# First conditioning chunks formed as columns, rotary tables made early, context keys moved behind u

## The chip, the core and the metric

The kernel runs on one core of a Trainium2 chip. The core has a matrix engine (TensorE, "PE" in the profile, with its weight loads as "PEld"), a vector engine (VectorE, DVE), an activation engine (ScalarE, ACT), a general engine (GpSimd, POOL) and a queue engine that issues the loads (SyncE, SP). They run side by side, each works through its own list of instructions in order, and they wait for each other by semaphores. The metric is the time of one execution on the device in microseconds (us). TensorE's clock has two levels, 1.2 and 2.4 GHz; the profile shows which of them was granted.

## The reference, cut to what matters

The model has two layers over 1024 tokens of width 1024, with a context of 256 tokens. Layer 0 is attention beside a spatial gating MLP, layer 1 a convolution module, and a SwiGLU FFN follows each. Every sub-layer is scaled and shifted by a conditioning vector (adaLN). The change lies in the beginning of layer 0:

```
def adaln(cvec, w_mod, b_mod):
    return jnp.split(jax.nn.silu(cvec) @ w_mod + b_mod, 6, axis=-1)
...
        sh1, sc1, gt1, sh2, sc2, gt2 = [t[:, None, :] for t in adaln(c, w_mod[l], b_mod[l])]
        xm = rms_norm(h, g_mix[l]) * (1.0 + sc1) + sh1
        if even or ctx_after:
            csh1, csc1, cgt1, csh2, csc2, cgt2 = adaln(c_ctx, w_mod[l], b_mod[l])
            xc = rms_norm(hc, g_mix[l]) * (1.0 + csc1) + csh1
...
    q, k, v, su, sv = split_in_proj(xm @ w_in)
    q = apply_axial_rope(rms_norm(q.reshape(b, n, N_Q_HEADS, HEAD_DIM), q_gain), rope)
    k = apply_axial_rope(rms_norm(k.reshape(b, n, N_KV_HEADS, HEAD_DIM), k_gain), rope)
```

Nothing of layer 0 can be projected before sh1 and sc1 are known: 2048 numbers each for `c` and for `c_ctx`, from an 8 MB part of `w_mod`.

## The kernel before

All activations lie transposed: 128 rows of the width on the partitions, tokens along the free side, the tokens in two halves A and B of 512. Each f32 operand of a large product is split into a high part (rounded to the engine's f32r format, on ACT, L112) and a low part (the rest, on DVE, L113), and a product is three matmuls over those parts (`mm3`, L175 to L181).

The beginning goes so. SP loads, in this order, the eight blocks of `w_mod` for sh1 and sc1 (`wma`, one 128 x 2048 block for each 128 rows k of the conditioning vector), half A of x among them (`xA`), then the first weights (`raw`), the context (`xc`) and half B (`xB`). For each block k, the two conditioning columns `s2v[:, k, :]` (for `c` and `c_ctx`) are multiplied with the block. Of its four chunks of 512 columns three go to TensorE, with the two conditioning columns as the stationary side, into three PSUM rows `mps` (L277). The fourth is done on DVE: it adds the block, weighted per partition, to two tiles `macc` (L278, L279, L254, L256), and TensorE sums these over partitions with a column of ones (L283 to L285). ACT copies the three rows out (`mrow`, L305), TensorE turns them into columns with 12 small transposes (L308), and all lands in `mcol`, 128 partitions x 16 columns x 2. DVE then makes the shift and scale (`mod`, `modc`, `gp`, L310 to L313), and half A, which was normalized meanwhile (`rbA`, L288), is shifted and split into `xm` (L387 to L403).

Then TensorE forms, in program order, keys and values of half A (`kv_tile` 2 to 5, tile `kvps`), of the context (0 and 1, from `xcm`), the first 256 columns of u for half A (`su_half(0, wu, 0)`, tile `ups`), keys and values of half B (6 to 9), u for half B, then queries (`qps`) and so on. Keys are turned by rotary tables `kC`, `kS` (`table`, L378, on POOL). Meanwhile DVE forms the later conditioning chunks (`adaln_group`: tile `acc` from `wmb` loads through a ring of three buffers, which the tiles of the sums of squares share).

The order of instructions on each engine is set at build time by the framework's scheduler, which starts from the order of the code and from its own estimate of when operands are there; so a small edit moves rows on every engine. Weight tiles `w` have four buffers, and blocks 4 to 7 of `wma` use the same four: a later weight can be split only when TensorE has finished with the block in its buffer.

Of the kernel before, what the change touches and what calls it, by code (L numbers as in the profile page):

```python
# [14 lines left out]
AF = mybir.ActivationFunctionType  # L15
ALU = mybir.AluOpType
AX = mybir.AxisListType

P = 128
D = 1024  # L20
KD = D // P
# [6 lines left out]
HD = 64  # L28
# [24 lines left out]
def hybrid_kernel(  # L53
# [19 lines left out]
    nc = tc.nc  # L73
# [15 lines left out]
    def htile(name="h", n=HALF):  # L89
        return hpool.tile([P, NB], F32, name=name, tag="h")[:, 0:n]  # L90
# [4 lines left out]
    def xtile(n=HALF, name="x"):  # L95
        return xpool.tile([P, NB], F32, name=name, tag="x")[:, 0:n]

    def blk(name="blk", dtype=F32R, n=HALF):
        return blkp.tile([P, 2, NB], dtype, name=name, tag="blk")[:, :, 0:n]

    def psa(n=HALF, name="psa"):
        return pa.tile([P, HALF], F32, name=name, tag="a")[:, 0:n]

    def psc(n=HALF, name="psc"):
        return pcn.tile([P, HALF], F32, name=name, tag="c")[:, 0:n]
# [15 lines left out]
    ident = const.tile([P, P], F32, name="ident")  # L121
# [27 lines left out]
    def prep(src):  # L149
        out = []  # L150
        for j in range(2):
            raw = load_raw(src[:, j * 1024:(j + 1) * 1024])
            w = wpool.tile([P, 2, 1024], F32R, name="w", tag="w")
            split(w[:, 0, :], w[:, 1, :], raw)
            out.append(w)
        return out
# [5 lines left out]
    def next_w():  # L162
        if not wready:
            wready.append(prep(wqueue.popleft()))
        w = wready.popleft()
        if wqueue:
            wready.append(prep(wqueue.popleft()))
        return w

    def w_rhs(w, k, c0=0, c1=256):  # L170
        t = w[k // 4]
        o = (k % 4) * 256
        return t[:, 0, o + c0:o + c1], t[:, 1, o + c0:o + c1]

    def mm3(ps, pairs):  # L175
        n = len(pairs) * 3
        i = 0
        for lh, ll, rh, rl in pairs:
            for a, b in ((lh, rh), (lh, rl), (ll, rh)):
                nc.tensor.matmul(out=ps, lhsT=a, rhs=b, start=(i == 0), stop=(i == n - 1))  # L180
                i += 1  # L181

    def col_sums(out, a):

        nc.tensor.matmul(out=out, lhsT=a, rhs=ones[:, 0:1], start=True, stop=True)


    def rstd_bcast(s, n, scale):

        at = [min(o, n - P) for o in range(0, n, P)]  # L190
        nj = len(at)
        ps = psc(nj, "ps_v")
        for j, o in enumerate(at):
            col_sums(ps[:, j:j + 1], s[:, o:o + P])
        v = sm(nj, "nv")
        nc.vector.tensor_scalar(out=v, in0=ps, scalar1=scale, scalar2=EPS, op0=ALU.mult, op1=ALU.add)  # L196
        r = rsqrt_small(v, nj, "nr")
        rb = psc(n, "rb")
        for j, o in enumerate(at):
            nc.tensor.matmul(out=rb[:, o:o + P], lhsT=r[:, j:j + 1].broadcast_to([P, P]), rhs=ident, start=True, stop=True)  # L200
        return rb

    def sumsq(tiles, n, alloc=ntile):
        s = None
        for t in tiles:
            q = alloc(n, "sq")
            nc.scalar.activation(q, t, AF.Square)
            if s is None:
                s = q
            else:  # L210
                nc.vector.tensor_tensor(out=s, in0=s, in1=q, op=ALU.add)
        return s
# [3 lines left out]
    def new_xm(half):  # L216
        xm[half] = [blk("xm") for _ in range(KD)]
# [15 lines left out]
    def load_pairs(half, k0, n):  # L233
        out = []
        for k in range(k0, k0 + n):
            if k % 2 == 0:
                t = blk("xp", F32)
            nc.sync.dma_start(out=t[:, k % 2, :], in_=xT[half, k])
            out.append(t[:, k % 2, :])
        return out  # L240
# [5 lines left out]
    s2 = const.tile([P, 16], F32, name="s2")  # L246
    nc.scalar.activation(s2, col(C_C2, 16), AF.Silu)
    s2v = s2.rearrange("p (k two) -> p k two", two=2)
    mps = [psa(name="mps") for _ in range(3)]
    macc = [xtile(name="macc") for _ in range(2)]  # L250

    def weighted_add(acc, w, cs, first):
        if first:
            nc.vector.tensor_scalar(out=acc, in0=w, scalar1=cs, scalar2=None, op0=ALU.mult)  # L254
        else:
            nc.vector.scalar_tensor_tensor(out=acc, in0=w, scalar=cs, in1=acc, op0=ALU.mult, op1=ALU.add)  # L256

    xA = []
    for k in range(KD):
        if k < 4:  # L260
            ws = []
            for i in range(2):
                t = blk("wma", F32)
                nc.sync.dma_start(out=t, in_=wm_a[k][:, i * 1024:(i + 1) * 1024].rearrange("p (a b) -> p a b", a=2))
                ws += [t[:, 0, :], t[:, 1, :]]
        else:
            t = wpool.tile([P, 2048], F32, name="wma", tag="w")
            nc.sync.dma_start(out=t, in_=wm_a[k])
            ws = [t[:, j * 512:(j + 1) * 512] for j in range(4)]
        if k in (1, 3):  # L270
            xA += load_pairs(0, 2 * (k - 1), 4)
        if k == 5:
            wqueue.append(w_in[2])
            wqueue.extend(w_in[{"q": 0, "u": 3, "v": 5}[kind] + g] for kind, g in STAGES)
            wqueue.extend(w_out[g] for _ in range(2) for g in range(4))
        for j in range(3):
            nc.tensor.matmul(out=mps[j][0:2, :], lhsT=s2v[:, k, :], rhs=ws[j], start=(k == 0), stop=(k == KD - 1))  # L277
        for e in range(2):  # L278
            weighted_add(macc[e], ws[3], s2v[:, k, e:e + 1], k == 0)  # L279
        if k == 4:  # L280
            rbA = rstd_bcast(sumsq(xA, HALF), HALF, 1.0 / D)
    mcol = psc(32, "mcol")
    for i in range(4):  # L283
        for e in range(2):
            col_sums(mcol[:, 24 + 2 * i + e:25 + 2 * i + e], macc[e][:, i * P:(i + 1) * P])  # L285
    wready.append(prep(wqueue.popleft()))
    for t in xA:
        nc.vector.tensor_tensor(out=t, in0=t, in1=rbA, op=ALU.mult)  # L288
# [1 line left out]
    for j in range(2):  # L290
        t = blk("xc", F32)
# [7 lines left out]
        nc.vector.scalar_tensor_tensor(out=gp[:, dst:dst + 8], in0=sc, scalar=1.0, in1=col(g, 8),  # L299
                                       op0=ALU.add, op1=ALU.mult)  # L300

    mrow = []
    for j in range(3):
        t = htile("mrow")
        nc.scalar.activation(t[0:2, :], mps[j][0:2, :], AF.Copy)  # L305
        mrow.append(t)
    for i in range(12):
        nc.tensor.transpose(mcol[:, 2 * i:2 * i + 2], mrow[i // 4][0:2, (i % 4) * P:(i % 4 + 1) * P], ident[0:2, 0:2])  # L308
    mcv = mcol.rearrange("p (i two) -> p i two", two=2)
    nc.vector.tensor_tensor(out=mod[:, 0:16], in0=mcv[:, :, 0], in1=col(C_BMOD, 16), op=ALU.add)  # L310
    nc.vector.tensor_tensor(out=modc, in0=mcv[:, :, 1], in1=col(C_BMOD, 16), op=ALU.add)
# [54 lines left out]
    kst2 = kvpool.tile([P, 2, NKT * P], F32R, name="kst2")  # L366
    v1 = kvpool.tile([P, NKT * 2, P], F32R, name="v1")
    v2 = kvpool.tile([P, NKT * 2, HD], F32R, name="v2")

    gt = htile("gt")  # L370
    nc.sync.dma_start(out=gt[:, 0:256], in_=gains.partition_broadcast(P))
    rt = []
    for i in range(2):
        t = htile("rt")
        nc.sync.dma_start(out=t, in_=rope[i])
        rt.append(t)

    def table(i, g):  # L378
        t = htile("tab")
        nc.gpsimd.tensor_tensor(out=t.rearrange("p (t d) -> p t d", d=HD),  # L380
                                in0=rt[i].rearrange("p (t d) -> p t d", d=HD),
                                in1=gt[:, g * HD:(g + 1) * HD].unsqueeze(1).broadcast_to([P, 8, HD]), op=ALU.mult)
        return t

    new_xm(0)

    def shift(k):  # L387
# [6 lines left out]
    def parts(k):  # L394
        t = xm[0][k]
        tc.keep_in_program_order(nc.scalar.activation(t[:, 0, :], xA[k], AF.Copy))
        nc.vector.tensor_tensor(out=t[:, 1, :], in0=xA[k], in1=t[:, 0, :].bitcast(F32), op=ALU.subtract)

    for k in range(0, KD, 2):
        shift(k)  # L400
        shift(k + 1)
        parts(k + 1)
        parts(k)  # L403
    kC, kS, qC, qS = table(0, 2), table(1, 3), table(0, 0), table(1, 1)
    xcm = [blk("xcm") for _ in range(4)]

    def xc_dst(k):
# [43 lines left out]
    def flush(n=0):  # L451
        while len(later) > n:
            later.popleft()()
# [44 lines left out]
    def su_half(g, wsu, half):  # L498
        for j in range(2):
            ps = psa(name="ups")  # L500
            mm3(ps, [(*w_rhs(wsu, k, j * P, (j + 1) * P), xm[half][k][:, 0, :], xm[half][k][:, 1, :])
                     for k in range(KD)])
            u = htile("u")
            nc.scalar.activation(u, ps, AF.Gelu_apprx_tanh)
            ut[2 * g + j, half] = u
# [10 lines left out]
    for kt in range(2, 6):  # L516
        kv_tile(kt)
    flush()
    for kt in range(0, 2):
        kv_tile(kt)  # L520
    flush()
    wu = next_w()
    su_half(0, wu, 0)
    for kt in range(6, 10):
        kv_tile(kt)
    flush()
# [212 lines left out]
    for n in range(len(steps) + LAG):  # L739
        if n < len(steps):  # L740
            i, kt = steps[n]
            while i not in prepped:
                next(bg)
            half, pair, e = units[i]
# [14 lines left out]
        i, kt = steps[n - LAG]  # L759
        half, pair, e = units[i]  # L760
# [33 lines left out]
    for half in range(2):  # L794
# [5 lines left out]
        for k in range(KD):  # L800
            t = htile("h")
# [399 lines left out]
```

## Time and profile before

| | |
|---|---|
| median of 3 runs | 2373.87 us (2371.97 to 2375.66) |
| profiled execution | 2372.76 us, its span 2371.0 us, mean granted clock 0.99 |
| busy of the span | PE 98%, PEld 83%, DVE 69%, ACT 39%, POOL 17% |

The span runs from the first to the last instruction; the profiled execution's own time is 1.76 us more. A busy PE is one with a matmul in flight. A matmul of this kernel in plain f32 leaves two records, called passes here: 24 matmuls into `mps` are 48 records.

### The profile page before, as it was taken

Reading aid. Unit: us, or ns where it says so; the run is one execution under the profiler, and the core shown is the slowest. Engines: PE = TensorE matmul, PEld = TensorE weight load, DVE = VectorE, ACT = ScalarE, POOL = GpSimd, SP = SyncE. Lnnn points to the kernel's source line nnn. Section 1 sums busy time; section 2 is a strip of 40 time slices with the busy share of each in tenths; the row PEclk is TensorE's granted clock in tenths of the full one; section 3 lists DMA queues with packets and bytes.
Section 4 is the critical chain, followed back from the end, with each engine's and each line's share of the span. In section 5 each row is a group of like instructions: output and inputs, shape, how many; then the busy total and the mean of one; then the engine's idle time right before and its main releaser. Section 6 shows DMA issues by size and latency. Waiting matters only on the chain.

```text
span 2371.0 us, 31670 instructions
## 1 busy us (share of the span) xinstructions
PE 2327.0 (98%) x12396; PEld 1978.2 (83%) x12396; DVE 1628.5 (69%) x2515; ACT 918.5 (39%) x1480; POOL 411.1 (17%) x405
## 2 busy tenths in 40 slices
PE   7999899999999999999999999999999999999998
PEld 3899677777888888888888788888878989999998
DVE  6887777656545666447999966999986555444357
ACT  4542688843211222234333455333445433222222
POOL 2362677820000000001112300002230000000000
PEclk9899999999999999999999999999999999999999
DMA  8451000042222455332222242222233222222222
GB/s 307 136 194 55 19 1 1 6 148 96 101 77 89 160 194 174 121 126 88 94 93 89 91 166 98 89 98 90 97 98 121 96 96 89 90 90 89 90 90 98
DMA packets 79573, 245.68 MB, mean 104 GB/s; under 512 B 8512, under 2 KB 12864, under 8 KB 78912
## 3 DMA queue, kind: packets, MB, share of 16 engines
q1 hardware_dynamic: 79424, 243.66, 30.4%
q8 instruction: 97, 1.59, 0.3%
q14 instruction: 52, 0.43, 0.1%
HBM read 235.24 MB, written 8.39 MB: 103 GB/s over the span
## 4 chain that ended last, share of the span: by engine, by line
PE 73%; DVE 12%; issue 2%; POOL 1%; ACT 1%; DMA 0%; DVEq 0%; ACTq 0%; POOLq 0%
PE gu L180 35%; PE fo L180 17%; PE pw L180 8%; DVE conv L999 7%; PE wo L180 4%; DVE w L113 2%; PE mx L628 2%; PE st L650 1%; PE st L649 1%; PE o L676 1%; PE o L674 1%; PE o L675 1%; POOL pacc L993 1%; DVE h L791 0%; DVE conv L1002 0%
## 5 line engine op out<-in xcount | busy, mean ns | idle before, releaser
L180 PE MATMUL gu<-xm,w 128*128 128x512 f32 (+2 forms) x5280 | 997.8, 350 | 1.9 <-ACT xm L226 1.9
L180 PEld LDWEIGHTS gu<-xm,w 128*128 128x128 f32 x5280 | 854.4, 188 | 135.0 <-ACT xm L226 2.1
L112 ACT ACTIVATE w<-raw 128x1024 fp32r<-128x1024 f32 x324 | 340.6, 1056 | 556.7 <-issue 237.7
L113 DVE TENSOR_TENSOR w<-raw,w 128x1024 fp32r<-128x1024 f32 x324 | 406.8, 1259 | 192.4 <-ACT w L112 191.8
L180 PE MATMUL fo<-act,w 128*128 128x512 f32 (+2 forms) x2640 | 499.8, 350 | 1.5 <-DVE act L113 1.5
L180 PEld LDWEIGHTS fo<-act,w 128*128 128x128 f32 x2640 | 428.3, 189 | 65.7 <-DVE act L113 1.9
L999 DVE SCALAR_TENSOR_TENSOR conv<-glu,pc,conv 128x496 f32<-128x496 f32 (+1 forms) x400 | 316.6, 836 | 0.3
L791 DVE SCALAR_TENSOR_TENSOR h<-fo,mod,h 128x264 f32<-128x264 f32 (+2 forms) x256 | 159.6, 631 | 96.7 <-PE fo L180 95.9
L993 POOL TENSOR_TENSOR pacc<-pacc,ptmp 128x496 f32<-128x496 f32 (+1 forms) x64 | 109.0, 1703 | 450.7 <-ACT pacc L989 398.3
L180 PE MATMUL pw<-xm,w 128*128 128x512 f32 x768 | 178.7, 394 | 0.0
L180 PEld LDWEIGHTS pw<-xm,w 128*128 128x128 f32 x768 | 144.1, 188 | 33.5
L841 DVE TENSOR_TENSOR silu<-gu,silu 128x512 f32<-128x512 f32 (+2 forms) x110 | 63.8, 580 | 141.0 <-PE gu L180 140.8
L840 ACT ACTIVATE silu<-gu 128x512 f32<-128x512 f32 (+2 forms) x110 | 56.2, 511 | 260.4 <-PE gu L180 260.4
L140 POOL TENSOR_TENSOR nr<-nv,mhalf 128x4 f32<-128x4 f32 (+2 forms) x16 | 16.4, 1027 | 803.3 <-DVE nv L196 803.3
L630 DVE TENSOR_REDUCE mp<-mx 128x1 f32<-128x512 f32 (+1 forms) x192 | 112.1, 598 | 24.6 <-PE mx L628 21.6
L112 ACT ACTIVATE act<-silu 128x512 fp32r<-128x512 f32 (+2 forms) x110 | 59.1, 537 | 143.6 <-DVE silu L841 143.6
L665 POOL TENSOR_TENSOR pb<-p,pb 128x512 fp32r<-128x512 f32 x80 | 104.3, 1304 | 5.3
L256 DVE SCALAR_TENSOR_TENSOR acc<-raw,s,acc 128x512 f32<-128x512 f32 x84 | 62.9, 749 | 45.2 <-DMA raw<-in_wm_b_dram 44.1
L180 PE MATMUL pw<-sw,w 128*128 128x264 f32 (+1 forms) x576 | 91.4, 320 | 0.0
L180 PE MATMUL wo<-cat,w 128*128 128x512 f32 x384 | 89.9, 394 | 0.7 <-DVE cat L113 0.7
L969 POOL MEMSET glu<- 128x15 f32 x16 | 0.9, 112 | 510.6 <-PE fo L180 510.6
L180 PEld LDWEIGHTS pw<-sw,w 128*128 128x128 f32 x576 | 83.0, 188 | 7.2
(169 smaller groups left out, 2450.3 us busy)
## 6 DMA issues: line engine op xcount, KB each, us to landing
raw<-in_ffn_in_dram SPq DMA_DIRECT2D x164, 512.0 KB, 3.6
raw<-in_ffn_out_dram SPq DMA_DIRECT2D x82, 512.0 KB, 3.6
raw<-in_wm_b_dram SPq DMA_DIRECT2D x48, 512.0 KB, 3.7
raw<-in_pw_dram SPq DMA_DIRECT2D x48, 512.0 KB, 3.7
wmb<-in_wm_b_dram SPq DMA_DIRECT2D x64, 256.0 KB, 2.8
raw<-in_w_out_dram SPq DMA_DIRECT2D x16, 512.0 KB, 3.6
raw<-in_w_in_dram SPq DMA_DIRECT2D x14, 512.0 KB, 4.6
wma<-in_wm_a_dram SPq DMA_DIRECT2D x8, 512.0 KB, 7.9
```

What stands on the lines that cost most here:

```text
L112: nc.scalar.activation(dst_hi, src, AF.Copy)
L113: nc.vector.tensor_tensor(out=dst_lo, in0=src, in1=dst_hi.bitcast(F32), op=ALU.subtract)
L180: nc.tensor.matmul(out=ps, lhsT=a, rhs=b, start=(i == 0), stop=(i == n - 1))
L256: nc.vector.scalar_tensor_tensor(out=acc, in0=w, scalar=cs, in1=acc, op0=ALU.mult, op1=ALU.add)
L628: pin(nc.tensor.matmul(out=ps, lhsT=b[:, 0, j * P:(j + 1) * P], rhs=kst1[:, kv, o:o + n], start=True, stop=True))
L630: chained(nc.vector.tensor_reduce(out=mp[:, 3 * j + s:3 * j + s + 1], in_=ps, axis=AX.X, op=ALU.max))
L665: chained(eng.tensor_tensor(out=t[:, 1, :], in0=p, in1=t[:, 0, :].bitcast(F32), op=ALU.subtract))
L791: nc.vector.scalar_tensor_tensor(out=h, in0=ps, scalar=gc, in1=h, op0=ALU.mult, op1=ALU.add)
L840: nc.scalar.activation(sg, ps, AF.Silu)
L841: nc.vector.tensor_tensor(out=sg, in0=ps, in1=sg, op=ALU.mult)
L993: nc.gpsimd.tensor_tensor(out=pacc, in0=pacc, in1=tmp, op=ALU.add)
L999: nc.vector.scalar_tensor_tensor(out=out, in0=g[:, t:t + n], scalar=wc(t), in1=out, op0=ALU.mult, op1=ALU.add)
```

## The change

It makes three edits. First, all 16 blocks of 128 columns of each `wma` block become the stationary side of a matmul, with the two conditioning columns as the moving side, so that TensorE writes columns into `mcol` at once: 16 matmuls with 2 moving columns for each k, 128 in all. The rows `mps`, the DVE tiles `macc`, the copies `mrow`, the transposes and the sums with ones go. Second, gains and rope are loaded, and the four rotary tables made, in step k = 1 of that loop. Third, the context's two key and value tiles come behind u of the first half.

```
-    mps = [psa(name="mps") for _ in range(3)]
-    macc = [xtile(name="macc") for _ in range(2)]
+    mcol = psc(32, "mcol")
...
+        if k == 1:
+            gt = htile("gt")
+            nc.sync.dma_start(out=gt[:, 0:256], in_=gains.partition_broadcast(P))
+            rt = []
+            for i in range(2):
+                t = htile("rt")
+                nc.sync.dma_start(out=t, in_=rope[i])
+                rt.append(t)
+            kC, kS, qC, qS = table(0, 2), table(1, 3), table(0, 0), table(1, 1)
...
-        for j in range(3):
-            nc.tensor.matmul(out=mps[j][0:2, :], lhsT=s2v[:, k, :], rhs=ws[j], start=(k == 0), stop=(k == KD - 1))
-        for e in range(2):
-            weighted_add(macc[e], ws[3], s2v[:, k, e:e + 1], k == 0)
...
+        for i in range(16):
+            nc.tensor.matmul(out=mcol[:, 2 * i:2 * i + 2], lhsT=ws[i // 4][:, (i % 4) * P:(i % 4 + 1) * P],
+                             rhs=s2v[:, k, :], start=(k == 0 and i == 0), stop=(k == KD - 1),
+                             skip_group_check=True)
...
-    mcol = psc(32, "mcol")
-    for i in range(4):
-        for e in range(2):
-            col_sums(mcol[:, 24 + 2 * i + e:25 + 2 * i + e], macc[e][:, i * P:(i + 1) * P])
...
-    mrow = []
-    for j in range(3):
-        t = htile("mrow")
-        nc.scalar.activation(t[0:2, :], mps[j][0:2, :], AF.Copy)
-        mrow.append(t)
-    for i in range(12):
-        nc.tensor.transpose(mcol[:, 2 * i:2 * i + 2], mrow[i // 4][0:2, (i % 4) * P:(i % 4 + 1) * P], ident[0:2, 0:2])
...
-    gt = htile("gt")
-    nc.sync.dma_start(out=gt[:, 0:256], in_=gains.partition_broadcast(P))
...
-    kC, kS, qC, qS = table(0, 2), table(1, 3), table(0, 0), table(1, 1)
...
+    wu = next_w()
+    su_half(0, wu, 0)
     for kt in range(0, 2):
         kv_tile(kt)
     flush()
-    wu = next_w()
-    su_half(0, wu, 0)
```

On TensorE the first rows were these, up to the first keys (names as above; `ps_v` and `rb` are the sum and the broadcast of a normalization, here that of half A; x counts matmuls that follow each other):

```order
L277 MATMUL mps<-wma,s_101 2x512 x12
L185 MATMUL ps_v<-ones,sq 128x1 x4
L277 MATMUL mps<-wma,s_101 2x512 x3
L200 MATMUL rb<-ident,nr 128x128 x4
L277 MATMUL mps<-wma,s_101 2x512 x9
L185 MATMUL mcol<-ones,macc 128x1 x8
L308 MATMUL mcol<-ident,mrow 128x2 x12
L180 MATMUL kvps<-w,xm 128x256 x30
```

and are now these (the two `ps_v` rows behind the first are those of the context and of half B):

```order
L296 MATMUL mcol<-s_101,wma 128x2 x80
L185 MATMUL ps_v<-ones,sq 128x1 x4
L296 MATMUL mcol<-s_101,wma 128x2 x15
L200 MATMUL rb<-ident,nr 128x128 x4
L296 MATMUL mcol<-s_101,wma 128x2 x33
L185 MATMUL ps_v<-ones,sq 128x1 x2
L180 MATMUL kvps<-w,xm 128x256 x8
L180 MATMUL ups<-xm,w 128x512
L200 MATMUL rb<-ident,nr 128x128 x2
L185 MATMUL ps_v<-ones,sq 128x1 x4
L180 MATMUL kvps<-w,xm 128x256 x72
```

24 wide matmuls, 8 sums and 12 transposes have become 128 matmuls of 2 columns; the normalization of half A stands in the same place among the blocks.

On DVE, around the making of `mod`, there stood before:

```order
L288 TENSOR_TENSOR xp<-xp,rb 128x512 x8
L256 SCALAR_TENSOR_TENSOR macc<-wma,s_101,macc 128x512 x2
L113 TENSOR_TENSOR w<-raw,w 128x1024 x2
L211 TENSOR_TENSOR sq<-sq 128x256 x2
L310 TENSOR_TENSOR mod<-mcol,pc 128x16
```

and now:

```order
L303 TENSOR_TENSOR xp<-xp,rb 128x512 x8
L211 TENSOR_TENSOR sq<-sq 128x512
L113 TENSOR_TENSOR w<-raw,w 128x1024
L211 TENSOR_TENSOR sq<-sq 128x512
L113 TENSOR_TENSOR w<-raw,w 128x1024
L211 TENSOR_TENSOR sq<-sq 128x512 x2
L253 TENSOR_SCALAR acc<-wmb,s_101 128x512
L318 TENSOR_TENSOR mod<-mcol,pc 128x16
```

The sums of squares of half B (`sq`, 128x512), two weight splits and the first step of a later conditioning chunk (`acc`, which needs a `wmb` load) stand ahead of `mod` now. That load is issued on SP behind the sixth `raw` load, and it waits for the last of those `sq` rows, whose buffer it takes.

Further down on DVE, the low parts of half B (`xm<-xp,mod,xm`) stood before like this:

```order
L225 SCALAR_TENSOR_TENSOR xp<-xp,gp,rb 128x512 x8
L256 SCALAR_TENSOR_TENSOR acc<-wmb,s_101,acc 128x512
L426 TENSOR_REDUCE ss<-kr 128x2
L113 TENSOR_TENSOR v_298<-kvps,v_297 128x64
L254 TENSOR_SCALAR acc<-wmb,s_101 128x512
L445 TENSOR_TENSOR qn<-qn,tab 128x128
L227 SCALAR_TENSOR_TENSOR xm<-xp,mod,xm 128x512 x5
```

and now the second of them has this ahead of it:

```order
L417 TENSOR_REDUCE ss<-kr 128x2
L255 SCALAR_TENSOR_TENSOR acc<-wmb,s_101,acc 128x512
L419 TENSOR_SCALAR hv<-ss 128x2
L436 TENSOR_TENSOR qn<-qn,tab 128x128
L437 TENSOR_TENSOR kr<-qn,kr 128x128
L255 SCALAR_TENSOR_TENSOR acc<-wmb,s_101,acc 128x512
L417 TENSOR_REDUCE ss<-kr 128x2
L113 TENSOR_TENSOR v_369<-kvps,v_368 128x64
L255 SCALAR_TENSOR_TENSOR acc<-wmb,s_101,acc 128x512
L436 TENSOR_TENSOR qn<-qn,tab 128x128
L419 TENSOR_SCALAR hv<-ss 128x2
L227 SCALAR_TENSOR_TENSOR xm<-xp,mod,xm 128x512
```

Between the normalized half B (`xp<-xp,gp,rb`) and the second of its eight low parts there are ten `acc` steps now; before, two stood ahead of the first five low parts. Behind the first queries TensorE's rows are the same as before.

## Rows read from the trace of the kernel before

**Rows 1.** The page: its first line, the span.

```profile
span 2371.0 us, 31670 instructions
```

**Rows 2.** Stretches: start:end, length, busy us (xcount) of each engine, granted clock, DMA.

```profile
28.90:42.40 13.50, 12.00 (x55) 5.09 (x54) 11.66 (x23) 6.25 (x12) 0.00 (x0) 1.00 1.04 405
42.60:49.30 6.70, 5.14 (x24) 5.14 (x25) 6.12 (x13) 6.70 (x14) 4.33 (x1) 0.50 0.51 200
...
63.80:68.80 5.00, 5.00 (x22) 4.77 (x22) 5.00 (x18) 2.15 (x8) 0.00 (x0) 0.50 0.16 50
68.80:70.60 1.80, 1.80 (x9) 1.77 (x8) 1.03 (x5) 0.45 (x2) 0.53 (x1) 0.50 0.37 125
70.60:76.60 6.00, 5.33 (x25) 5.24 (x26) 3.86 (x10) 1.37 (x6) 3.31 (x7) 0.50 0.55 186
76.70:113.00 36.30, 36.30 (x219) 31.85 (x218) 32.02 (x75) 19.91 (x53) 15.06 (x25) 1.00 0.42 138
```

**Rows 3.** Timeline of PE, 5 to 46 us: start, us, instruction, xcount [idle before].

```profile
5.94 8.20 PE L277 MATMUL mps<-wma,s 128*2 128x512 f32 x12 [5.94 <-DMA wma<-in_wm_a_dram]
...
30.30 7.89 PE L277 MATMUL mps<-wma,s 128*2 128x512 f32 x18
38.12 1.95 PE L185 MATMUL mcol<-ones,macc 128*128 128x1 f32 x16
...
44.16 6.13 PE L180 MATMUL kvps<-w,xm 128*128 128x256 f32 x30 [3.26 <-ACT xm L396]
```

**Rows 4.** Timeline of PE, 63 to 77 us.

```profile
63.75 5.12 PE L180 MATMUL kvps<-w,xcm 128*128 128x256 f32 x22 [2.57 <-DVE xcm L227]
68.86 1.84 PE L185 MATMUL ps_v<-ones,sq 128*128 128x1 f32 x8
...
75.60 1.55 PE L200 MATMUL rb<-ident,nr 128*128 128x128 f32 x8
```

**Rows 5.** Passes with one moving column: shortest/median/longest ns, first and last start.

```profile
L185 PE MATMUL ps_v<-ones,sq x112: 164/250/353, 23.9 to 2361.5; 128*128 128x1 f32 x112
```

**Rows 6.** Timeline of PE, first queries and what follows.

```profile
112.97 4.17 PE L180 MATMUL qps<-w,xm 128*128 128x256 f32 x33
...
136.73 23.04 PE L180 MATMUL qps<-w,xm 128*128 128x256 f32 x192
...
159.96 22.48 PE L180 MATMUL ups<-xm,w 128*128 128x512 f32 x96
```

**Rows 7.** Timeline of DVE and POOL around the making of mod.

```profile
40.94 0.17 DVE L310 TENSOR_TENSOR mod<-mcol,pc 128x16 f32<-128x16 f32 x1 [0.95 <-PE mcol L308]
44.97 10.11 POOL L380 TENSOR_TENSOR tab<-rt,gt 128x512 f32<-128x512 f32 x4 [17.96 <-DMA rt<-in_rope_dram]
```

**Rows 8.** Groups of ACT and DVE, 0 to 45 us: busy us, mean ns | idle before.

```profile
L112 ACT ACTIVATE w<-raw 128x1024 fp32r<-128x1024 f32 x2 | 2.1, 1058 | 10.3 <-DMA raw<-in_w_in_dram 10.3
L207 ACT ACTIVATE sq<-xp 128x512 f32<-128x512 f32 x8 | 5.0, 629 | 14.2 <-DMA xp<-in_xT_dram 13.7 <-DVE sq L211 0.2
L113 DVE TENSOR_TENSOR w<-raw,w 128x1024 fp32r<-128x1024 f32 x2 | 2.4, 1220 | 0.0
L256 DVE SCALAR_TENSOR_TENSOR macc<-wma,s,macc 128x512 f32<-128x512 f32 x14 | 9.9, 748 | 6.6 <-DMA wma<-in_wm_a_dram 6.6
```

**Rows 9.** DMA issues: xcount, KB each, median us from issue to landing.

```profile
wmb<-in_wm_b_dram SPq DMA_DIRECT2D x64, 256.0 KB, 2.8
raw<-in_w_in_dram SPq DMA_DIRECT2D x14, 512.0 KB, 4.6
```

**Rows 10.** Timeline of SP and DVE: the third raw load's issue, a sq, the acc steps.

```profile
37.42 0.33 SPq L146 DMA_DIRECT2D raw<-in_w_in_dram  x1
...
68.04 0.68 DVE L211 TENSOR_TENSOR sq<-sq 128x512 f32<-128x512 f32 x1
...
69.43 0.49 DVE L254 TENSOR_SCALAR acc<-wmb,s 128x512 f32<-128x512 f32 x1
...
73.83 0.75 DVE L256 SCALAR_TENSOR_TENSOR acc<-wmb,s,acc 128x512 f32<-128x512 f32 x1 [1.12 <-DMA wmb<-in_wm_b_dram]
```

More of the change, by code (lines that the diff above doesn't have):

```diff
@@ L258, in hybrid_kernel, with table @@
     xA = []
+    def table(i, g):
+        t = htile("tab")
+        nc.gpsimd.tensor_tensor(out=t.rearrange("p (t d) -> p t d", d=HD),
+                                in0=rt[i].rearrange("p (t d) -> p t d", d=HD),
+                                in1=gt[:, g * HD:(g + 1) * HD].unsqueeze(1).broadcast_to([P, 8, HD]), op=ALU.mult)
+        return t
     for k in range(KD):
@@ L368, in hybrid_kernel @@
     v2 = kvpool.tile([P, NKT * 2, HD], F32R, name="v2")
-    gt = htile("gt")
-    nc.sync.dma_start(out=gt[:, 0:256], in_=gains.partition_broadcast(P))
[L372 to L383, printed above, removed]
     new_xm(0)
```

## The prediction, made before the changed kernel ran

> **What bounds the kernel now.** I read the page first: a span of 2371.0 us [rows 1], to which the profiled execution adds 1.76, 2372.76 in all. The busy shares of the page say little, because TensorE is waited for nearly everywhere. So I asked for stretches of the beginning. From 76.7 us TensorE is busy without a break and at the full clock [rows 2], and the first queries start at 112.97 [rows 6]. Behind them TensorE's rows are unchanged. So what the change is worth is the shift of one event, the first query, and I cost everything ahead of it.
>
> Ahead of it there are two parts. Up to 40.94, where `mod` is made [rows 7], the conditioning chunks are formed. Keys start at 44.16 [rows 3], 3.2 us behind `mod`. From there to the first query it takes 68.8 us. How much of that is work? At the full clock a key or query pass costs 23.04 / 192 = 0.120 us and a u pass 22.48 / 96 = 0.234 [rows 6]. The stretch holds 240 passes for keys and values, 96 for u and some 40 narrow ones (norms, transposes) at about 0.11 (below): 28.8 + 22.5 + 4.3, say 55 us. So 14 us are lost to waits (2.57 us for the context's low parts alone [rows 4]) and to the half clock, which was granted from 42.6 to 49.3 and from 63.8 to 76.6 [rows 2].
>
> **The new conditioning part.** 24 wide matmuls are replaced by 128 with two moving columns. They are plain f32, so 256 passes, each with 128x128 weights of its own. The trace has this form with one moving column. Eight such passes took 1.84 us at the half clock; the longest such pass of the trace lasted 0.353, so one starts every (1.84 - 0.353) / 7 = 0.213 us. At the full clock 16 took 1.95, with a median of 0.250, so one every 0.113 [rows 3 to 5]. These are the two bounds of the price. A second column is another column of streaming, which I neglect.
>
> Here the Trainium skill can be weighed against the rows. "TensorE: Matmul & The Clock Gate", section on LDWEIGHTS, gives a load by its columns alone, an estimate of 107 ns for 128 columns. By that the passes would cost 27 us at either level. The rows agree at 2.4 GHz (0.113) and not at 1.2 GHz (0.213).
>
> So the granted clock decides. At the start it is the half one: the first twelve passes of `mps` took 8.20 us, eighteen later ones 7.89 [rows 3]. Then wide passes raised it. Would narrow ones? From 63.75 to 70.7 TensorE worked almost without a gap, 22 recorded key passes of 256 columns and then the eight narrow ones [rows 4], and the clock stayed at 0.50 [rows 2]. From 44.16 on, 256-column passes without the narrow ones raised it within 5.2 us, and from 71 to 76.6 key passes and eight passes of 128 columns did too [rows 2, 4]. And before 42.4 it was full under `mps`, and fell after narrow sums, small transposes and a wait of 3.26 us [rows 2, 3]. I take it that narrow passes don't raise it, so the price is 0.213.
>
> The order on TensorE puts 8 `ps_v` and 8 `rb` passes among the 256, which run at the same half clock and price. Thus the columns are ready at 5.94 + 272 x 0.213 = 63.9 us, against 40.9 before: **+23.0**. No load holds this up: the gains and rope loads (128 KB and twice 256 KB by their shapes) ahead of block 2 take 1.6 us at the 405 GB/s of rows 2, and TensorE, which came to block 7 at 30.30 + 12 x 0.44 = 35.6 before [rows 3], now does at 57.1.
>
> What goes is worth little here. DVE loses 16 `macc` steps of about 0.7 us [rows 8], and ACT its copies, but these lay beside loads and TensorE. The tables' 10.1 us on POOL [rows 7] move from 45 to 55 us into a time when POOL has nothing to do.
>
> **From the columns to the keys.** `mod` now stands on DVE behind `acc`. That needs the first `wmb` load, which waits for the last `sq` of half B, and that one stands behind a weight split whose buffer TensorE frees 32 passes before the end, at 57.1. From there: split on ACT 1.06, low part on DVE 1.22, `sq` add 0.68, square 0.63, add 0.68 [rows 8, 10] make 61.4; load 2.8 [rows 9], `acc` 0.49 [rows 10]: 64.7. That is **+0.8** behind the columns (bounds: 0 if the load is early, 3.8 if it starts only when the columns are ready). With 3.2 us from `mod` to the keys as before, keys start at 68.0.
>
> **From the keys to the first query.** 55 us of work at the full clock. TensorE comes to it at half clock. Before, the first such spell lasted 5.2 us behind the first key and the second 13.7, of which half each is lost. Now the first nine key and u matmuls are followed by twelve passes for norms, eight of them narrow, so I take 9 us at half, **4.5** lost (bounds 2.6 and 6.8, half of each spell). Context keys behind u no longer wait for `xcm`: DVE has its low parts ready some 10 us before. What is late next is half B. Ten `acc` steps now stand between its normalization and its second low part. Half B's `rb` stands behind some 80 key passes, at about 85 us; eight steps of 0.68 (taken as long as the `sq` add) bring DVE to 90. With three buffers, load 2.8 and step 0.75 [rows 9, 10], three `acc` steps take 3.6 us at best; three loads have landed by then, the other seven steps take some 9 us, and each waits in the same row of instructions for keys to be finished. So the low parts come at 102 to 108, and TensorE asks at 103 (the first query less 96 key passes and 48 of u): **2.5** (bounds 0, since before there was no such wait, and 5). Together 68.0 + 55 + 4.5 + 2.5 = 130, against 112.97, or 17 us later. The second part gains 7 us of the 14 lost; the first loses 24.
>
> **The sum.** 2372.76 + 17 = 2389.8. The profiled execution lies 1.1 below the median, which is within the runs' own spread, so I forecast **2390**.
>
> **Rivals.**
> First, the clock does rise under narrow passes. The Trainium skill says so if read plainly: "TensorE: Matmul & The Clock Gate", in the table under "Why this matters for your kernels", asks only that TensorE be kept busy without a pause. No row here has a long run of narrow passes, so only the 1.84 us in rows 4 speak against it. Then, with 27 passes at half until about 11.7, the columns are ready at 5.94 + 27 x 0.213 + 245 x 0.113 = 39.4. But then the load of `wmb` decides: the third `raw` load, issued at 37.42 before [rows 10] and now 1.6 later for the rope, lands at some 43.6 with 4.6 us of landing [rows 9]; split, sums, load and `acc` as above (1.06 + 1.22 + 1.99 + 2.8 + 0.49) make 51.2, keys at 54.4, the first query at 54.4 + 55 + 5 = 114.4. That gives +1.5, **2374**: no difference. The point from which it decides is the pass time: below about 0.15 us the change is no longer slower.
> Second, on the faster side, the clock rises and the load of `wmb` is early: keys at 39.4 + 3.2 = 42.6, the first query at 42.6 + 55 + 3 = 100.6, so **2360**. Against it speaks the order on DVE and SP, where `sq` and the sixth `raw` load come first.
> Third, slower than forecast: the wait for half B lets the clock fall once more, as after the 3.26 us in rows 3; 5 us of wait and 3 at half clock give **2396**.
>
> **How the numbers follow.** About 0.2%, 4.7 us, is what a measurement of this kernel can tell. Half clock, the forecast: 0.84, the third rival within it (0.12). The first rival: 0.12, most of it within 0.2%. The second: 0.04, faster. So faster 0.04, same 0.11, slower 0.85. With the bounds (0 to 3.8, 2.6 to 6.8, 0 to 5) the forecast's case reaches from 2385 to 2397; a clock that rises for part of the run lies below. I give 2378 to 2398, which leaves out the two fast rivals.
>
> **What would show it.** Right: granted clock 0.50 until some 70 us, `mcol` passes every 0.213, the last at 64, keys at 68, the first query near 130, and the same distances behind it. Wrong: `mcol` passes every 0.113, or `mod` waiting for a `wmb` load for long, or half B's low parts in time. If the first query comes before 118, my reading of the clock has failed.

## The result, and the profile after

The changed kernel took 2388.9 us (median of 4 runs, 2388.30 to 2390.72), the kernel before in the same session 2372.97 (2371.97 to 2375.66): ratio 1.0067, 95% interval 1.0049 to 1.0084. It is 15.9 us slower. The forecast was 2390, and slower.

The profiled execution has this span, on the page's first line; it is 16.0 us longer than before's [rows 1]:

```profile
span 2387.0 us, 31992 instructions
```

The timeline of TensorE up to the first query (start, us, instruction, xcount, idle before) answers to [rows 3, 4, 6]:

```profile
5.45 34.26 PE L296 MATMUL mcol<-s,wma 128*128 128x2 f32 x160 [5.45 <-DMA wma<-in_wm_a_dram]
...
49.53 14.08 PE L296 MATMUL mcol<-s,wma 128*128 128x2 f32 x66
...
66.50 2.08 PE L180 MATMUL kvps<-w,xm 128*128 128x256 f32 x8 [2.04 <-ACT xm L388]
...
70.44 8.79 PE L180 MATMUL kvps<-w,xm 128*128 128x256 f32 x72
...
87.99 5.82 PE L180 MATMUL ups<-xm,w 128*128 128x512 f32 x24 [0.69 <-ACT u L495]
...
94.50 4.73 PE L180 MATMUL kvps<-w,xcm 128*128 128x256 f32 x38 [0.69 <-ACT u L495]
...
102.88 0.62 PE L180 MATMUL kvps<-w,xm 128*128 128x256 f32 x3 [1.78 <-DVE xm L227]
...
103.87 6.20 PE L180 MATMUL kvps<-w,xm 128*128 128x256 f32 x38 [0.27 <-DVE xm L227]
...
128.39 0.49 PE L180 MATMUL qps<-w,xm 128*128 128x256 f32 x2
```

The first 160 recorded `mcol` passes take 34.26 us, one every 0.213, without a gap. The last ends at 49.53 + 14.08 = 63.6. Keys start at 66.50 (44.16 before), and the first query follows at 128.39: 15.4 us later than before's 112.97. The same holds further on: the first score pass of the attention is 16.0 us later, and the end 16.0.

What stands ahead of `mod`, and ahead of half B's low parts, on SP and DVE (answers to [rows 7, 10]):

```profile
61.18 3.89 SPq L331 DMA_DIRECT2D wmb<-in_wm_b_dram  x3
...
63.76 0.49 DVE L253 TENSOR_SCALAR acc<-wmb,s 128x512 f32<-128x512 f32 x1 [2.64 <-DMA wmb<-in_wm_b_dram]
64.16 0.17 DVE L318 TENSOR_TENSOR mod<-mcol,pc 128x16 f32<-128x16 f32 x1
...
100.15 0.75 DVE L255 SCALAR_TENSOR_TENSOR acc<-wmb,s,acc 128x512 f32<-128x512 f32 x1 [2.73 <-DMA wmb<-in_wm_b_dram]
...
102.07 0.75 DVE L227 SCALAR_TENSOR_TENSOR xm<-xp,mod,xm 128x512 fp32r<-128x512 f32 x1
```

`mod` does stand behind `acc`, which waited 2.64 us for the first `wmb` load; but the load landed as the columns were ready, so the gate cost half a microsecond. At 102 us the second low part of half B stands behind an `acc` step that waited 2.73 us for its load. TensorE's waits of 1.78 and 0.27 us are there.

Stretches, with the granted clock behind the busy times (answers to [rows 2]):

```profile
103.80:107.00 3.20, 3.13 (x14) 3.13 (x15) 3.04 (x8) 2.52 (x7) 1.59 (x2) 0.50 0.08 30
260.80:274.30 13.50, 11.91 (x30) 8.45 (x31) 9.48 (x15) 8.52 (x14) 8.53 (x8) 0.50 0.11 41
```

The clock fell to half for 3.4 us right behind the wait for half B. At the start of the attention it was half for 13.7 us, where before it was so for 6.8. This trace's first record of the clock, at the full level, starts at 69.6; that it was the half one until then is read from the passes, 0.213 apart.

### The profile page after: what moved, and what is told of

It reads as the page before. It is cut to its first block, busy times and chain, and to the rows that moved or that the text cites. A ratio compares the mean times of both kernels' runs of the same rounds, so it can differ in the third digit from the quotient of the medians.

```text
span 2387.0 us, 31992 instructions
## 1 busy us (share of the span) xinstructions
PE 2349.8 (98%) x12576; PEld 2023.2 (85%) x12576; DVE 1613.2 (68%) x2499; ACT 917.7 (38%) x1477; POOL 419.9 (18%) x405
## 3 DMA queue, kind: packets, MB, share of 16 engines
q8 instruction: 98, 1.61, 0.3%
## 4 chain that ended last, share of the span: by engine, by line
PE 80%; DVE 6%; POOL 1%; issue 1%; ACT 1%; DMA 0%; DVEq 0%; POOLq 0%; ACTq 0%
PE gu L180 37%; PE fo L180 18%; PE pw L180 11%; PE wo L180 4%; DVE conv L990 3%; PE mx L619 1%; PE st L641 1%; PE st L640 1%; PE o L667 1%; PE o L665 1%; PE o L666 1%; DVE w L113 1%; POOL pacc L984 1%; PE ps_v L185 0%; PE rb L200 0%
## 5 line engine op out<-in xcount | busy, mean ns | idle before, releaser
L984 POOL TENSOR_TENSOR pacc<-pacc,ptmp 128x496 f32<-128x496 f32 (+1 forms) x64 | 119.7, 1870 | 439.4 <-ACT pacc L980 389.1
L621 DVE TENSOR_REDUCE mp<-mx 128x1 f32<-128x512 f32 (+1 forms) x192 | 112.3, 599 | 25.6 <-PE mx L619 22.4
L211 DVE TENSOR_TENSOR sq<-sq 128x512 f32<-128x512 f32 (+3 forms) x112 | 64.1, 572 | 46.0 <-ACT sq L207 43.3
```

The costliest lines, as they stand in the source:

```text
L621: chained(nc.vector.tensor_reduce(out=mp[:, 3 * j + s:3 * j + s + 1], in_=ps, axis=AX.X, op=ALU.max))
L984: nc.gpsimd.tensor_tensor(out=pacc, in0=pacc, in1=tmp, op=ALU.add)
```

## The experiments

All times of one table row are medians; the kernel before lay at 2373.0 to 2373.3 in each session. Of my twelve expected ranges only that of e9_tables was met; the other eleven kernels came out 0.2 to 7.6 us above theirs. So what follows rests on the rows and on which kernel was faster, and not on my numbers.

| kernel | us | ratio, 95% interval |
|---|---|---|
| changed (columns, tables early, context behind u) | 2388.9 | 1.0067 (1.0049 to 1.0084) |
| e1_wide: changed, chunk passes 128 columns wide | 2377.3 | 1.0015 (1.0006 to 1.0024) |
| e2_rows: rows, tables early, context behind u | 2373.4 | 0.9999 (0.9991 to 1.0008) |
| e3_chunks: columns alone | 2398.7 | 1.0104 (1.0089 to 1.0120) |
| e4_ctx: rows, context behind u alone | 2377.5 | 1.0018 (1.0010 to 1.0027) |
| e5_chunks_ctx: columns, context behind u | 2392.1 | 1.0079 (1.0065 to 1.0092) |
| e6_after_accB: changed, `acc` behind half B | 2394.6 | 1.0089 (1.0073 to 1.0104) |
| e7_rows_accB: e2_rows, `acc` behind half B | 2371.5 | 0.9994 (0.9985 to 1.0003) |
| e8_wide_accB: e1_wide, `acc` behind half B | 2376.3 | 1.0012 (1.0004 to 1.0021) |
| **e9_tables: rows, tables early alone** | **2369.6** | **0.9983 (0.9974 to 0.9991)** |
| e10_rows_acc1: as e7, second `acc` group only | 2371.7 | 0.9997 (0.9988 to 1.0005) |
| e11_mixed: 3/4 rows, 1/4 columns, else as e2 | 2377.6 | 1.0017 (1.0008 to 1.0026) |
| e12_mixed_accB: e11, `acc` behind half B | 2376.0 | 1.0011 (1.0003 to 1.0020) |

**Is the price the clock? (e1_wide, e11_mixed)**

e1_wide keeps passes and weights, and only repeats the two moving columns:

```diff
-    mcol = psc(32, "mcol")
+    mwide = [psa(name="mwide") for _ in range(4)]
...
-            nc.tensor.matmul(out=mcol[:, 2 * i:2 * i + 2], lhsT=ws[i // 4][:, (i % 4) * P:(i % 4 + 1) * P],
-                             rhs=s2v[:, k, :], start=(k == 0 and i == 0), stop=(k == KD - 1),
+            nc.tensor.matmul(out=mwide[i // 4][:, (i % 4) * P:(i % 4 + 1) * P],
+                             lhsT=ws[i // 4][:, (i % 4) * P:(i % 4 + 1) * P],
+                             rhs=s2v[:, k, :].unsqueeze(1).broadcast_to([P, 64, 2]),
+                             start=(k == 0 and i % 4 == 0), stop=(k == KD - 1),
...
```

> The changed kernel with the moving side of the chunk passes repeated to 128 columns (the same two columns 64 times); the same 256 passes with the same weights, in four PSUM tiles instead of one. My theory (the price is the half clock, which passes of two moving columns don't raise): the clock rises in these passes, one then starts every 0.113 us, the columns are ready between 39 and 42 us instead of 63.6, keys start at about 45 (or at 54 if a wmb load holds mod), the first query at 102 to 114, the time is 2360 to 2374. Rival (a pass with weights of its own costs 0.213 us at the start of the kernel whatever the clock, or the 64 times larger streaming costs as much): columns at 64 or later, 2388 or more.

Stretches of e1_wide with the granted clock, and its timeline of TensorE:

```profile
28.10:34.10 6.00, 6.00 (x29) 6.00 (x30) 0.16 (x1) 0.00 (x0) 1.03 (x1) 0.50 1.01 423
35.60:46.40 10.80, 10.80 (x97) 10.62 (x96) 9.73 (x22) 4.94 (x10) 0.00 (x0) 1.00 1.04 406
```

```profile
52.30 1.23 PE L200 MATMUL rb<-ident,nr 128*128 128x128 f32 x4 [4.45 <-POOL nr L140]
53.17 6.21 PE L180 MATMUL kvps<-w,xm 128*128 128x256 f32 x32
...
88.69 4.62 PE L180 MATMUL kvps<-w,xm 128*128 128x256 f32 x24 [2.44 <-DVE xm L227]
```

The same passes with the same weights cost 6.0 / 29 = 0.207 us at half clock and 10.8 / 97 = 0.111 at full, within one kernel. With 64 times the columns the chunks were ready at 46.4 us, 17.2 earlier than in the changed kernel, and the time fell by 11.6. The rival is out. My number was too low, though. The columns came at 46.4 and not by 42 (loads held the passes, and from 27.3 to 34.1 the clock was half), and the first key only at 53.17. What holds it is not `wmb`, as I had thought possible, but the context's norm, which stands ahead of the key on TensorE and waits 4.45 us, most of them for POOL (below). Half B's low parts took 2.44 more at 88.69.

e11_mixed goes the other way: the narrow form stays, between wide passes. Against e2_rows (below), which has the chunks as rows:

```diff
-    macc = [xtile(name="macc") for _ in range(2)]
+    mcx = psa(8, "mcx")
...
-        for e in range(2):
-            weighted_add(macc[e], ws[3], s2v[:, k, e:e + 1], k == 0)
+        for i in range(4):
+            nc.tensor.matmul(out=mcx[:, 2 * i:2 * i + 2], lhsT=ws[3][:, i * P:(i + 1) * P], rhs=s2v[:, k, :],
+                             start=(k == 0 and i == 0), stop=(k == KD - 1), skip_group_check=True)
...
```

> Early tables and context's keys behind u, and of each chunk three quarters as rows (wide passes) and the last quarter as columns (64 narrow passes between the wide ones) in place of the macc steps on DVE. My theory (narrow passes cost little where wide ones keep the clock up, and DVE is free of 16 steps of 0.7 us): columns ready at 39 to 42 us, 2367 to 2372. Rival (narrow passes among wide ones go at 0.213 all the same, or the context's norm ahead of the first key on TensorE delays the keys as in the kernel with wide passes): 2374 to 2379.

Its timeline of TensorE, and the stretch in which the chunks are formed:

```profile
41.88 1.05 PE L299 MATMUL mcx<-s,wma 128*128 128x2 f32 x8
...
49.82 1.23 PE L200 MATMUL rb<-ident,nr 128*128 128x128 f32 x4 [4.19 <-POOL nr L140]
50.69 5.01 PE L180 MATMUL kvps<-w,xm 128*128 128x256 f32 x32
```

```profile
8.60:43.00 34.40, 30.15 (x127) 12.73 (x126) 13.79 (x23) 10.91 (x20) 6.30 (x5) 1.00 1.03 399
```

Eight narrow passes take 1.05 us here, where eight of one column at half clock took 1.84 [rows 4]: between wide passes the clock stays up, and the narrow form costs little more than half as much. With e1_wide, the forecast's step is shown from both sides: the price is the clock's, and in the changed kernel narrow passes by themselves didn't raise it. Whether a long row of them would let a clock fall that wide passes had raised was not run. The time missed my range for the reason in e1_wide: the first key waits for the context's norm and starts at 50.69. A gain from the relief of DVE does not show.

**Which part does what? (e2_rows to e5, e9_tables)**

e2_rows is the changed kernel with the chunks as in the kernel before; e3_chunks is the reverse, the kernel before with the diff's hunks on `mcol` alone; e4_ctx and e9_tables are the kernel before with one other hunk each, below in this order; e5_chunks_ctx is e3_chunks with e4_ctx's:

```diff
+    wu = next_w()
+    su_half(0, wu, 0)
     for kt in range(0, 2):
         kv_tile(kt)
     flush()
-    wu = next_w()
-    su_half(0, wu, 0)
```

```diff
+        if k == 1:
+            gt = htile("gt")
...
+            kC, kS, qC, qS = table(0, 2), table(1, 3), table(0, 0), table(1, 1)
...
-    kC, kS, qC, qS = table(0, 2), table(1, 3), table(0, 0), table(1, 1)
```

> The changed kernel with the chunks formed as rows and macc sums as before; early tables and the context's keys behind u stay. My theory (all of the loss is in the chunks): mod near 42 us, keys near 45, no wait for xcm, so the first query 2 to 8 us earlier than before's 112.97 and a time of 2365 to 2371. Rival (the move of the tables or of the context's keys costs too, by later loads or by the wait for half B's low parts): 2373 to 2378.

> The kernel before with the chunks formed as columns, and nothing else changed. My theory: columns ready at 62 to 64 us, the wait for the context's low parts is as before or hidden, and the time is that of the whole change or a few us more, 2387 to 2397. Rival (the other two moves cost, not the chunks): near 2373.

> The kernel before with only the context's keys moved behind u of the first half. My theory: the 2.57 us wait for xcm goes and a half-clock spell gets shorter, so 2366 to 2371, unless half B's low parts are late, which takes up to 5 us back. Rival (the order of keys has no part in it, or half B is late): 2372 to 2377.

> Chunks as columns and the context's keys behind u, tables late as before: the changed kernel without its second part. Chunks alone took 2398.7. My theory (the move of the context's keys gives 8 to 10 us of that back, because the keys' evictions and norms no longer hold u; the tables lie under other work either way): 2387 to 2390, first query near 128. Rival (the early tables give it back): 2395 to 2400, first query near 137.

> The kernel before with only the tables made early. With the context's keys behind u, the early tables were worth 4.2 us with rows (2377.5 to 2373.4) and 3.2 with columns (2392.1 to 2388.9). My theory (late tables hold POOL for 10 us and the loads for half B's norm): 2 to 4 us less than before, 2369 to 2372. Rival (with the context's keys ahead of u POOL holds nothing up, and the rope loads delay mod by 1.6 us): 2373 to 2376.

The columns are the loss: alone they cost 25.6 us, and without them (e2_rows) it is gone. The rival of e3_chunks is out. But both smaller parts have effects that I had not seen.

The context's keys behind u gave 6.6 us back with columns (2398.7 to 2392.1; less than expected) and cost 4.4 with rows, where I had expected a gain. Timeline of TensorE in the kernel before, then in e4_ctx:

```profile
77.69 4.57 PE L180 MATMUL ups<-xm,w 128*128 128x512 f32 x19
...
88.92 2.30 PE L180 MATMUL kvps<-w,xm 128*128 128x256 f32 x18
```

```profile
68.15 8.07 PE L180 MATMUL ups<-xm,w 128*128 128x512 f32 x22 [3.24 <-ACT u L504]
...
81.17 1.05 PE L200 MATMUL rb<-ident,nr 128*128 128x128 f32 x8
...
85.95 0.98 PE L180 MATMUL kvps<-w,xm 128*128 128x256 f32 x6 [1.52 <-ACT xm L226]
...
91.26 5.88 PE L180 MATMUL kvps<-w,xm 128*128 128x256 f32 x35 [4.32 <-DVE xm L227]
```

Before, half B's norm (`rb` at 75.60 [rows 4]) is followed by 11 us of u, and in that time DVE normalizes half B: its keys start at 88.92 without a wait. In e4_ctx u has been used up ahead of the context's keys, `rb` comes at 81.17, and half B's keys wait 1.52 and 4.32 us; u itself waits 3.24 for an eviction. The 2.57 us wait is gone, and others of 9 have come. With columns, half B's `rb` comes in time (84.20 in e5_chunks_ctx, ahead of 11 us of u), so the move does not take its cover. There the old order is the bad one. DVE and TensorE in e3_chunks:

```profile
87.52 2.06 DVE L225 SCALAR_TENSOR_TENSOR xp<-xp,gp,rb 128x512 f32<-128x512 f32 x3
...
94.69 0.17 DVE L416 TENSOR_SCALAR hv<-ss 128x2 f32<-128x2 f32 x1
```

```profile
96.24 5.42 PE L180 MATMUL kvps<-w,xcm 128*128 128x256 f32 x24 [6.81 <-ACT qn L421]
```

Half B's normalization stands on DVE ahead of the norms of the context's keys (`hv` at 94.69), and TensorE waits 6.81 us for the `qn` behind them.

The early tables gave 4.2 us (e4_ctx to e2_rows), 3.2 (e5_chunks_ctx to the changed kernel) and 3.7 alone (e9_tables), which is faster than before and the best kernel of the study. I had costed them at nothing. The four tables in the kernel before take 10.1 us on POOL [rows 7], and in the changed kernel, where DVE has little to do beside them, 5.3:

```profile
14.77 5.33 POOL L262 TENSOR_TENSOR tab<-rt,gt 128x512 f32<-128x512 f32 x4 [9.56 <-DMA rt<-in_rope_dram]
```

What else they did shows in DVE's rows. The timeline of DVE in the kernel before:

```profile
48.88 1.65 DVE L113 TENSOR_TENSOR w<-raw,w 128x1024 fp32r<-128x1024 f32 x1 [0.58 <-ACT w L112]
50.46 1.77 DVE L211 TENSOR_TENSOR sq<-sq 128x512 f32<-128x512 f32 x1
52.15 1.78 DVE L397 TENSOR_TENSOR xm<-xp,xm 128x512 fp32r<-128x512 f32 x1
...
53.93 1.70 DVE L397 TENSOR_TENSOR xm<-xp,xm 128x512 fp32r<-128x512 f32 x1
...
56.69 0.68 DVE L397 TENSOR_TENSOR xm<-xp,xm 128x512 fp32r<-128x512 f32 x1
```

Steps that take 0.68 take 1.70 to 1.78 until the tables end at 55.1, and a weight split, 1.22 by [rows 8], takes 1.65. Four such rows are 0.43 + 1.09 + 1.10 + 1.02 = 3.6 us longer than their kind; in e9_tables the same steps take their usual 0.68 and 1.22. TensorE's side of it, in e9_tables, and a stretch with the granted clock behind the busy times:

```profile
59.55 2.86 PE L180 MATMUL kvps<-w,xcm 128*128 128x256 f32 x18 [0.54 <-DVE xcm L227]
...
109.70 4.40 PE L180 MATMUL qps<-w,xm 128*128 128x256 f32 x35
```

```profile
65.50:72.20 6.70, 6.60 (x31) 6.63 (x32) 3.39 (x11) 1.38 (x6) 3.47 (x6) 0.50 0.55 194
```

The wait for the context's low parts is 0.54 instead of 2.57, and the first query comes 3.3 us earlier. But waits of 0.64 and 1.76 follow, so that TensorE waits only 1.1 us less in all between the first key and the first query, a stretch that is 3.8 us shorter. Beside the rest of that stands the second half-clock spell, 6.8 us long here and 13.7 before (63.0 to 76.6). So DVE's 3.6 us are not the 3.7 of the two medians one for one: the chain from shorter steps to shorter waits and a shorter spell is read from one execution of each kernel.

**Is half B late by `acc`? (e6, e7, e8, e10, e12)**

```diff
             a = weighted_add(acc, w, s2v[:, k, 0:1], k == 0)
+            if g < 2 and k == 0:
+                tc.add_manual_dep(a.ins, lowB.ins.name, mybir.DependencyInfo(
+                    mybir.DependencyClass.NoSync, mybir.DependencyReason.DATA), reason="order")
```

`lowB` is the last low part of half B; in e10_rows_acc1 the condition is `g == 1`.

> The changed kernel with the first two groups' acc steps ordered behind the last low part of half B on DVE. My theory (the waits of 1.78 and 0.27 us for half B and the fall of the clock behind them come from the acc steps and their loads): both go, mod no longer waits for a wmb load, so 2 to 5 us less than the changed kernel, 2384 to 2387. Rival (half B is late by its norm, not by acc, or the wmb loads now hold the weights' loads): 2388 to 2393.

> Chunks as rows, early tables, context's keys behind u, and the acc steps behind half B as above. Before this order of acc TensorE waited 1.75, 3.17 and 1.30 us between the context's keys and half B's. My theory (with rows the gain of moving the context's keys is lost to DVE, which is busy 95% there): 3 to 6 us of these go, 2367 to 2371, faster than the kernel before. Rival (half B's norm is late on TensorE and POOL, and acc only fills DVE's gaps): 2372 to 2375.

> Chunk passes with the moving side repeated to 128 columns, and the acc steps behind half B as above. Wide passes alone took 2377.3, with 2.44, 1.08 and 1.69 us of waits between the context's keys and the last keys. My theory as in the kernel with rows: 3 to 5 us less, 2372 to 2375. Rival: 2376 to 2379.

> Chunks as rows, early tables, context's keys behind u, and only the second acc group ordered behind half B; the first stays in DVE's gaps. With both groups behind half B the first query came 4.9 us earlier than in the kernel before, but 1.84 us of wait for acc and a fall of the clock among the queries took most of it back. My theory: the late wait goes and a part of the early gain stays, 2368 to 2371.5. Rival (acc of the first group holds half B again): 2372 to 2374.

> As the mixed kernel, with the first two acc groups behind half B on DVE. My theory: 1 to 3 us less than the mixed kernel, 2365 to 2371, faster than before. Rival (the acc work is late among the queries instead): as the mixed kernel or 2 us more.

In e6_after_accB TensorE no longer waits for half B, so the wait was `acc`'s. But the kernel took 5.7 us more. Its timeline of POOL, TensorE and DVE:

```profile
67.20 4.62 POOL L140 TENSOR_TENSOR nr<-nv,mhalf 128x2 f32<-128x2 f32 x1 [22.30 <-DVE nv L196]
...
71.88 1.22 PE L200 MATMUL rb<-ident,nr 128*128 128x128 f32 x4 [1.80 <-POOL nr L140]
...
124.83 7.39 PE L180 MATMUL ups<-xm,w 128*128 128x512 f32 x24 [2.00 <-ACT u L501]
...
161.82 0.63 PE L349 MATMUL adps<-ident,acc 128*128 128x128 f32 x4 [2.22 <-DVE acc L257]
```

The norm's two numbers took 4.62 us on POOL instead of 1.61, TensorE waited 1.80 for them, and u waited 2.00 more behind its eviction; the clock fell there once more. The first query came at 132.05, 3.7 us later than in the changed kernel, and behind it TensorE waited 2.22 more, for the `acc` that had been put off. In e7_rows_accB the first query did come early, and the lead was lost among the queries:

```profile
108.07 1.10 PE L180 MATMUL qps<-w,xm 128*128 128x256 f32 x8
...
143.67 0.63 PE L361 MATMUL adps<-ident,acc 128*128 128x128 f32 x4 [1.84 <-DVE acc L258]
```

4.9 us ahead at 108.07, then a wait of 1.84 for the `acc` that had been put off, a fall of the clock behind it, and narrow passes that before lay ahead of the first query. What is left is 1.9 us, which can't be told from nothing. e10_rows_acc1, meant to mend this, came out the same, with its first query late again (114.95); e8_wide_accB came out 1.0 us under e1_wide and e12_mixed_accB 1.6 under e11_mixed, both less than the spread of their runs, with late waits for `acc` of 3.10 and 2.72. In these orders, to move the `acc` steps moved the waits.

## Why the prediction was right

**The clock, and the columns at 63.9.** Right, measured 63.6, and shown by e1_wide and e11_mixed. The ground for it was thin, 1.84 us of narrow passes in [rows 4]. The Trainium skill ("TensorE: Matmul & The Clock Gate", "Why this matters for your kernels") asks that TensorE be kept busy without a pause; the trace after does not agree that this is enough, since 34.26 us of narrow passes without a gap stayed at 0.213.

**`mod` 0.8 behind the columns, keys 3.2 behind `mod`.** Measured 0.5 and 2.3. Both are smaller, so keys started at 66.5 and not at 68.0. With the tables late (e5_chunks_ctx) they started at 68.17.

**From the keys to the first query 62.** Measured 61.9, but by terms that partly cancel. The half clock behind the first key was 3.1 us long and not 9 (66.50 to 69.6), so 1.5 lost instead of 4.5. In e5_chunks_ctx it was 9 (keys at 68.17, the first record of the full clock at 77.4), and the timeline of TensorE shows it in the 72 passes that took 8.79 us after:

```profile
72.88 10.79 PE L180 MATMUL kvps<-w,xm 128*128 128x256 f32 x72
```

What makes the difference stays open. The wait for half B was 2.05 (forecast 2.5) and, as the third rival said, let the clock fall: 1.7 more. And u's second half and the first context key each waited 0.69 for an eviction of `u`, which I had not foreseen: 1.4. Together 1.5 + 2.05 + 1.7 + 1.4 = 6.7, against 7.0. That is luck: 3.0 too much for the half clock against 3.1 for what I had left out.

**"What goes is worth little", and the tables at nothing.** This is the term that failed, by 3 to 4 us (3.2 in the changed kernel). I looked at when POOL had time, and not at what the tables did to DVE beside them.

**"The second part gains 7 us of the 14 lost; the first loses 24."** As stretches of time this held: up to the keys 22.3 were lost (44.16 to 66.50), and from the keys to the first query 6.9 gained (68.8 to 61.9). By edits it splits otherwise, and I had not foreseen how: columns alone cost 25.6, and the other two edits gave 9.8 of it back, 6.6 by the context's keys and 3.2 by the tables. This holds beside the columns only. I had counted the wait that goes (2.57) as a gain, and in the kernel before its removal uncovers half B and costs 4.4.

**The sum.** 2388.9 against 2390, near the middle of the range of 2378 to 2398. The columns came 0.3 us earlier than forecast, the keys 1.5 and the first query 1.6; the larger errors, of 3 us, lay behind the keys and cancelled.

**The rivals.** The first rival's condition, a full clock in the chunks, was made in e1_wide: keys at 53.17 (worked out: 54.4), the first query at 116.7 (114.4), 2377.3 (2374). It would not have been faster either, though it was another wait that decided. The second rival, 2360, came from no kernel.

## What to carry to other kernels

A pass with two moving columns and weights of its own cost as much here as one with 128, at either clock (0.213 and 0.207 us at half, about 0.11 at full); so a row of 256 of them at the start of the kernel, where the clock stayed at half, cost double, and the same passes between wide ones did not. A block that covers another's norm (u here) is worth more than the wait in front of it: before moving work behind it, ask what it covers now. And a step on an engine with time to spare is not free while the engine beside it is busy: look at its neighbours' durations in that stretch, not only at its own idle time.

## What the runs showed of the hardware

POOL and DVE hold each other up, in both directions. The tables on POOL made two-operand steps on DVE 2.5 times as long (1.70 to 1.78 us instead of 0.68). It is not the `TENSOR_TENSOR` steps alone: in e9_tables, where the tables end at 20.49, the first two `macc` steps beside them (`SCALAR_TENSOR_TENSOR`) took 3.10 us together, where one takes 0.75 [rows 8]:

```profile
14.75 5.74 POOL L263 TENSOR_TENSOR tab<-rt,gt 128x512 f32<-128x512 f32 x4 [9.54 <-DMA rt<-in_rope_dram]
17.95 3.10 DVE L256 SCALAR_TENSOR_TENSOR macc<-wma,s,macc 128x512 f32<-128x512 f32 x2 [2.69 <-DMA wma<-in_wm_a_dram]
```

And POOL's `nr`, on two numbers, waits for `TENSOR_TENSOR` steps on DVE to end. DVE and POOL in e6_after_accB, after, e11_mixed and e9_tables:

```profile
68.17 3.09 DVE L394 TENSOR_TENSOR xm<-xp,xm 128x512 fp32r<-128x512 f32 x5
```

```profile
66.46 1.22 DVE L113 TENSOR_TENSOR w<-raw,w 128x1024 fp32r<-128x1024 f32 x1
66.63 1.61 POOL L140 TENSOR_TENSOR nr<-nv,mhalf 128x2 f32<-128x2 f32 x1 [22.81 <-DVE nv L196]
```

```profile
46.88 2.88 POOL L140 TENSOR_TENSOR nr<-nv,mhalf 128x2 f32<-128x2 f32 x1 [18.24 <-DVE nv L196]
...
48.52 0.68 DVE L400 TENSOR_TENSOR xm<-xp,xm 128x512 fp32r<-128x512 f32 x1
```

```profile
50.85 1.28 DVE L401 TENSOR_TENSOR xm<-xp,xm 128x512 fp32r<-128x512 f32 x2
51.01 1.08 POOL L140 TENSOR_TENSOR nr<-nv,mhalf 128x2 f32<-128x2 f32 x1 [22.80 <-DVE nv L196]
```

In e6_after_accB DVE's row ends at 71.26 and `nr` at 71.82; after, 67.68 and 68.24; in e11_mixed, 49.20 and 49.76. It is 0.56 us each time, whether `nr` began 1.05 or 4.06 us ahead of that. But it does not always wait for the whole row: in e9_tables the first of two `xm` steps ends at 51.53, and `nr` 0.56 behind it, at 52.09, while the second still runs. In the changed kernel the next step on DVE is an `acc`, and `nr` runs beside it too. What decides how many steps go first stays open. Where several do, TensorE is left waiting for `nr`: it took 2.88 us within the wait of 4.19 in e11_mixed and within that of 4.45 in e1_wide, and 4.62 ahead of that of 1.80 in e6_after_accB.

The Trainium skill ("SBUF — State Buffer", "SBUF: two separate sides") has a port pair that DVE and GpSimd take by an exclusive lock, so that the other blocks. The rows agree that one holds up the other; which of several waiting steps comes next, they leave open. That the tables slow DVE is shown by e9_tables; that DVE holds `nr` is read from these coincidences alone, since no kernel that keeps such steps away from `nr` was run.
